# End of the mixers in a hybrid decoder block: the last step's closing traced ahead of the output projection, results stored by GpSimd's queue, the next norm taken operand by operand

## The chip, the cores and the metric

The kernel runs on one core of a Trainium2 chip. A core has five engines with instruction streams of their own: PE (TensorE, matrix products), DVE (VectorE), ACT (ScalarE), POOL (GpSimd) and SP (SyncE, which here only issues transfers). Transfers (DMAs) run on 16 DMA engines that all queues share. The metric is the device time of the whole kernel in microseconds (us). A difference of 0.3%, 9 us, is about what a measurement of this kernel can tell from no change.

## The reference

One decoder layer over 1024 tokens of width 1024, behind 16 meta tokens that are dropped at the end. All is float32.

```
h = [meta; x]
h = h + 0.5 * swiglu(rmsnorm(h), ...)             # first feed-forward block, inner width 2816
u = rmsnorm(h) @ w_in                             # one input projection for both mixers
o_a = gated DeltaNet (8 heads of 128, short causal convolution, chunks)
o_b = RWKV-7 time mixing (16 heads of 64)
h = h + (sigmoid(ga) * o_a + sigmoid(gb) * o_b) @ w_out
h = h + 0.5 * swiglu(rmsnorm(h), ...)             # second feed-forward block
out = rmsnorm(h)[16:]
```

## The kernel before, in words

Activations are kept transposed: 8 row blocks of 128 channels by tokens. Every float32 operand of a large product is split into a high part (`fp32r`, written by ScalarE, L163) and the rest (written by VectorE, L164), and a product is the three matmuls high x high, high x low and low x high. A weight block of 128 x 1024 is loaded into one of two buffers `wraw` by SP, split into one of two buffers `w`, and used by 24 matmuls (`mm3`, L301 to L308; L307 is the matmul).

The kernel has three stages: `ffn1`, `middle` (the mixers) and `ffn2`. The mixers go through two halves of the tokens ("segments", `s` 0 and 1) and in each through 8 channel blocks `j`: 16 steps. The parts of a step (`merge_blocks`, `transitions`, `chains`, `gates`, `finish` and those that prepare later steps) are called in the order of strings such as `FINAL` (L192), which holds for the last step. That order is how the program is written; a scheduler that records all calls then merges them into one instruction stream per engine, by its own estimates of what will be ready. It never reorders on the chip: each engine works through its stream, and a waiting instruction holds all behind it.

The parts around the change:

- `chains` (L1701): short dependent products; the last ones are `bq` (L1773).
- `finish` (L1808) closes a step: square of `oa` and of `yb`, each split into one buffer `hl` (L1226 to L1228), two column sums on TensorE for each (`cs`, L1213), logarithm and exponential (`ro`, `rg`, L1232 and L1234), then VectorE scales and adds (L1815 to L1823). The result `yb` goes to memory (`mdr`) for all steps but the last, whose `yb` is split at once into the operand tile `uk`.
- `fill` (L1035) is the output projection of segment 0. It has no dependence on the last step and fills TensorE beside it. `wout` (L1095) takes a row block `ho` of `h` from memory (L1041), runs 24 matmuls into `pwo` (L307), adds (L1101), and the sum is stored to `h2dr` (L1045). Then it loads the seven merged operands `mr` of segment 1 that lie in memory (L1090) and splits them into `uk` tiles; there are eight of those, so each is free when the last product of segment 0 has read it. `ho` and `mr` share one ring of eight slots (`tmp_tile`), so `mr` number k waits for store number k to have read its slot.
- `ffn2` (L880) loads `h` of segment 0 back from `h2dr` and that of segment 1 from `hdr` into tiles `hh` (L894), whose first 512 columns hold segment 0. `first_half` (L375) runs the norm of segment 0: squares (L320), sums on VectorE (L327), one sum over partitions on TensorE (`nps`, L338), logarithm and exponential (`nrs`, L340 and L341), then per row block a scaling (L381) and a split into `b`. Then the output projection of segment 1 runs (`wout` again, eviction at L1101 into the second 512 columns of `hh`, store to `h3dr`, L898), and `start` runs the norm of segment 1 (squares L363, sums on TensorE L365) beside the first products `pg` of the feed-forward block (L518, later L494).

Of the kernel before, what the change touches and what calls it, by code (L numbers as in the profile page):

```python
# [15 lines left out]
KD = D // P  # L16
# [21 lines left out]
NJ = 8  # L38
# [150 lines left out]
BEFORE_SWITCH = "merge_blocks transitions operands+ inverses+ chains gates finish banks gates+ segment decay++ new_b++ tokens++ new_a++"  # L189
SWITCH = "merge_blocks transitions operands+ inverses+ chains finish decay++ new_b++ new_a++"  # L190
LAST_BUT_ONE = "merge_blocks transitions operands+ inverses+ chains gates finish"
FINAL = "gates merge_blocks transitions chains fill finish"  # L192


def weight_order():
# [179 lines left out]
def first_half(g, hs, gname, n, b, on_pe):  # L375

    src = lambda k: hs[k][:, :n]
    rs = rstd(g, src, n, on_pe)
    yield
    for k in range(KD):  # L380
        g.nc.vector.scalar_tensor_tensor(src(k), src(k), g.V(gname, k), rs, op0=ALU.mult, op1=ALU.mult)  # L381
        bk = b["21" if k >= HK else "11"][:, k % HK]
        split(g, src(k), bk[:, 0, :], bk[:, 1, :])
    yield


def second_half(g, hs, gname, n, b):
# [381 lines left out]
def ffn1(g):  # L769
    tc, nc = g.tc, g.nc  # L770
    n = T // 2
    with ExitStack() as ctx:
# [12 lines left out]
        with tc.tile_pool(name="f1n", bufs=1, reuse_waits="tile") as sp:  # L785
            hs = [sp.tile([P, T], F32, name=f"h{k}") for k in range(KD)]
            for s in range(2):
                for k in range(KD):
                    sl = slice(s * n, (s + 1) * n)
                    (nc.sync if s or k % 2 else nc.scalar).dma_start(hs[k][:, sl], g.a["hT"][k][:, sl])  # L790
                if not s:
                    weight_tiles(g)
                    q0 = whole(g, 1, 0, 0, g.wq[0], g.wq[1])
                    w0 = next(q0)
            q1 = whole(g, 1, 0, 1, g.wq[4], g.wq[2], g.wq[3])
            w1 = next(q1)
            first = first_half(g, hs, "g1", n, b, True)
            next(first)
            next(q0)
            next(first)  # L800
            next(q0)
            start(g, 1, hs, "g1", n, b, (w0, w1), q1)
            gu = g.gate_up
# [76 lines left out]
def ffn2(g):  # L880
    tc, nc = g.tc, g.nc
    n = FULL
    main_banks(g, 1, 6, 8)
    with ExitStack() as ctx:
# [4 lines left out]
        g.ga = ctx.enter_context(tc.tile_pool(name="ga", bufs=1, reuse_waits="tile"))  # L889
        with tc.tile_pool(name="f2n", bufs=1, reuse_waits="tile") as sp:  # L890
            hs = [sp.tile([P, SEQ], F32, name=f"hh{k}") for k in range(KD)]
            for s in range(2):
                for k in range(KD):
                    nc.sync.dma_start(hs[k][:, s * n : (s + 1) * n], g.hdr[1][k] if s else g.h2dr[k])  # L894
            for _ in first_half(g, hs, "g2", n, b, False):
                pass
            for m, ho in wout(g, g.mg, lambda m: hs[m][:, n:]):
                nc.sync.dma_start(g.h3dr[m], ho)  # L898
            g.upctx.close()
            cp = ctx.enter_context(tc.tile_pool(name="f2c", bufs=1, side="right", reuse_waits="tile"))  # L900
            pools.update({x: cp for x in ("t2", "t3", "22", "t4", "t1")})
            b.update({x: cp.tile([P, HK, 2, n], F32R, name=f"b{x}", tag=f"b{x}", bufs=1) for x in pools if x not in b})
            g.wx = right.enter_context(tc.tile_pool(name="wx", bufs=1, side="right", reuse_waits="tile"))
            b["12"] = b["t4"]
            weight_tiles(g)
            q0 = whole(g, 2, 0, 0, g.wq[0], g.wq[1])
            q1 = whole(g, 2, 0, 1, g.wq[4], g.wq[2], g.wq[3])
            w = next(q0), next(q1)
            next(q0)
            next(q0)  # L910
            start(g, 2, hs, "g2", n, b, w, q1)
            gu = g.gate_up
# [122 lines left out]
def fill(g, q):  # L1035

    nc = g.nc

    def add(m):
        ho = tmp_tile(g, "ho")[:, :FULL]  # L1040
        nc.sync.dma_start(ho, g.hdr[0][m][:, SEGS[0][2] :])  # L1041
        return ho

    for m, ho in wout(g, merged(g, 0, range(NJ)), add):
        nc.sync.dma_start(g.h2dr[m], ho)  # L1045
    g.mg = merged(g, 1, range(NJ - 1))


def tmp_tile(g, name, w=528):
# [758 lines left out]
def finish(g, q):  # L1808

    nc, st, V, j = g.nc, g.st, g.V, q.j  # L1810
    oa, yb, zg, gg = q.oa, q.yb, q.zg, q.gg
    sq = q.Va.rearrange("p c m -> p (c m)")
    ro = st.tile([P, FULL], F32, name="ro", tag="ro")
    colsum_rsqrt(g, "ones", oa, sq, ro, FULL, 1.0 / P, V("eps"), pool="ch")
    nc.vector.tensor_tensor(oa, oa, ro, op=ALU.mult)  # L1815
    nc.vector.scalar_tensor_tensor(oa, oa, V("aog"), zg, op0=ALU.mult, op1=ALU.mult)
    sq = q.AR[:, 0:4].rearrange("p c y m -> p (c y m)")
    rg = st.tile([P, FULL], F32, name="rg", tag="ro")
    colsum_rsqrt(g, "bd", yb, sq, rg, FULL, 1.0 / 64, V("gneps"), pool="ch")
    nc.vector.scalar_tensor_tensor(yb, yb, V("lng", j), rg, op0=ALU.mult, op1=ALU.mult)  # L1820
    nc.vector.scalar_tensor_tensor(yb, yb, V("lnb", j), q.bv, op0=ALU.add, op1=ALU.add)
    nc.vector.tensor_tensor(yb, yb, gg, op=ALU.mult)
    nc.vector.tensor_tensor(yb, yb, oa, op=ALU.add)  # L1823
    if q.it + 1 < 2 * NJ:
        nc.sync.dma_start(g.mdr[q.s][j], yb)
    else:
        g.mg.append(u_tile(g, yb))


ACTIONS = {"new_b": new_b, "tokens": tokens, "new_a": new_a, "operands": operands, "inverses": inverses, "merge_blocks": merge_blocks, "transitions": transitions,  # L1830
# [88 lines left out]
```

## Time and profile before

| | |
|---|---|
| median of three runs | 3006.02 us (3003.01 to 3011.42) |
| profiled execution, its own time | 3009.62 us |
| its span in the profile | 3007.6 us |
| TensorE busy | 2890.0 us, 96% of the span |
| VectorE / ScalarE / GpSimd busy | 73% / 48% / 16% |
| DMA, mean | 111 GB/s |
| last step's `bq` to the first `pg` of the second feed-forward block | 2276.9 to 2350.8 us |

A row of the timeline reads: start in us from the span's start, length in us, engine, line, operation, tile written <- tiles read, shape, count, and in brackets the idle time ahead of it with the instruction that ended it. A row of the chain of waits reads: start, length, what; the chain is followed back from the last instruction, at each step to what released it. A float32 product that is no `fp32r` product (the norms' sums) has two rows for each matmul. An instruction's length includes its tail, in which the next may start; where a pace is wanted, starts are compared. SPq and POOLq are transfers at their issue; the data lands later.

### The profile page before, as it was taken

The numbers are of one execution on the slowest core, as the hardware profiler recorded it, in microseconds if no ns is written. First come the engines' busy times: TensorE is split into PE (matmuls) and PEld (weight loads), VectorE is DVE, ScalarE is ACT, GpSimd is POOL, SyncE is SP. The second block draws the span as 40 slices with busy tenths as digits, with TensorE's granted clock in tenths as the row PEclk, the third lists the DMA queues.
The fourth block names the chain that finished last, engine by engine and source line by source line (L and its number), as shares of the span: only waits on it lengthen the run. The fifth ranks groups of instructions, "written<-read, shape, count | busy, mean of one in ns | idle before, by whom it ended". The sixth has DMA issues, their size and how long they took to land.

```text
span 3007.6 us, 62829 instructions
## 1 busy us (share of the span) xinstructions
PE 2890.0 (96%) x25630; PEld 2501.7 (83%) x25630; DVE 2194.8 (73%) x4079; ACT 1445.0 (48%) x2546; POOL 491.2 (16%) x554
## 2 busy tenths in 40 slices
PE   8999999998989999999998999999998999999998
PEld 8999999998878888888776777777776888888886
DVE  7566668776667877788767887777866666667886
ACT  5322234345655656566566656656644432223444
POOL 0332332323000000000000100100100033332531
PEclk9999999999999999999999999999999999999999
DMA  3433236453232322333332332233354333333762
GB/s 123 134 107 106 93 122 210 170 193 111 74 74 66 83 72 64 81 82 87 93 90 71 81 82 75 74 84 86 106 148 158 114 109 103 100 104 132 248 226 95
DMA packets 286849, 333.14 MB, mean 111 GB/s; under 512 B 172432, under 2 KB 178576, under 8 KB 286560
## 3 DMA queue, kind: packets, MB, share of 16 engines
q1 hardware_dynamic: 284752, 325.77, 35.7%
q8 instruction: 201, 3.29, 0.5%
q10 hardware_dynamic: 1728, 3.16, 0.3%
q14 instruction: 88, 0.72, 0.1%
q0 software_dynamic: 80, 0.19, 0.0%
HBM read 261.67 MB, written 67.38 MB: 109 GB/s over the span
## 4 chain that ended last, share of the span: by engine, by line
PE 50%; DVE 12%; ACT 5%; issue 2%; DMA 1%; SPq 0%; POOL 0%; DVEq 0%; ACTq 0%
PE pp L307 16%; PE pg L494 11%; PE pd L707 6%; PE pwo L307 3%; DVE w L164 2%; DVE tb L1581 1%; PE pg L518 1%; DVE Xb L1583 1%; ACT w L163 1%; PE cs L1213 1%; PE vp L1266 1%; PE mp L1266 1%; DVE mt L1689 1%; PE gra L1467 1%; PE np L1266 1%
## 5 line engine op out<-in xcount | busy, mean ns | idle before, releaser
L307 PE MATMUL pp<-uk,w 128*128 128x512 f32 (+2 forms) x4824 | 969.8, 347 | 15.2 <-DVE h L714 6.0
L307 PEld LDWEIGHTS pp<-uk,w 128*128 128x128 f32 x4824 | 744.0, 191 | 111.9 <-DVE w L164 13.1
L707 PE MATMUL pd<-form,w 128*128 128x256 f32 (+2 forms) x2772 | 437.2, 320 | 9.9 <-DVE w L164 9.2
L707 PEld LDWEIGHTS pd<-form,w 128*128 128x128 f32 x2772 | 396.7, 190 | 49.9 <-DVE w L164 12.3
L494 PE MATMUL pg<-bt,w 128*128 128x256 f32 (+2 forms) x2520 | 401.7, 318 | 2.5 <-DVE w L164 2.0
L164 DVE TENSOR_TENSOR w<-wraw,w 128x1024 fp32r<-128x1024 f32 (+2 forms) x266 | 349.2, 1313 | 74.9 <-ACT w L163 71.8
L494 PEld LDWEIGHTS pg<-bt,w 128*128 128x128 f32 x2520 | 360.2, 188 | 36.4 <-DVE w L164 3.1
L163 ACT ACTIVATE w<-wraw 128x1024 fp32r<-128x1024 f32 (+2 forms) x266 | 276.5, 1040 | 191.5 <-PE pg L494 116.1
L500 DVE TENSOR_TENSOR c<-c,pg 128x520 f32<-128x520 f32 (+1 forms) x280 | 189.5, 689 | 240.0 <-PE pg L494 216.0
L494 PE MATMUL pg<-b,w 128*128 128x256 f32 (+2 forms) x2160 | 347.9, 318 | 0.0
L494 PEld LDWEIGHTS pg<-b,w 128*128 128x128 f32 x2160 | 309.8, 188 | 28.0
L163 ACT ACTIVATE w<-wrx 128x1024 fp32r<-128x1024 f32 (+1 forms) x64 | 58.4, 912 | 280.4 <-PE pg L494 238.5
L464 POOL TENSOR_TENSOR wrx<-wrx 128x512 f32<-128x512 f32 x38 | 52.5, 1382 | 727.0 <-DVE w22b L164 549.8
L164 DVE TENSOR_TENSOR form<-form 128x520 fp32r<-128x520 f32 (+1 forms) x152 | 145.1, 991 | 13.0 <-ACT form L163 12.7
L163 ACT ACTIVATE w<-wsum 128x768 fp32r<-128x768 f32 x96 | 75.7, 788 | 160.3 <-PE pd L707 120.9
L164 DVE TENSOR_TENSOR w<-wsum,w 128x768 fp32r<-128x768 f32 x96 | 116.0, 1214 | 36.8 <-ACT w L163 36.8
L1583 DVE TENSOR_TENSOR Xb<-Xb,tb 115x126 f32<-115x126 f32 (+22 forms) x496 | 125.8, 254 | 8.9 <-DVE tb L1581 0.2
L163 ACT ACTIVATE form<-form 128x520 fp32r<-128x520 f32 (+1 forms) x152 | 94.2, 632 | 77.1 <-DMA form<-frm 67.7
L1581 DVE TENSOR_TENSOR tb<-Ub,Xb 115x126 f32<-115x126 f32 (+22 forms) x496 | 124.5, 251 | 8.4 <-DMA Ub<-scr 1.2
L242 POOL TENSOR_TENSOR wsum<-wsum,wraw 128x768 f32<-128x768 f32 (+1 forms) x48 | 96.3, 2020 | 209.7 <-DMA wraw<-in_wdn 122.1
L1390 DVE SCALAR_TENSOR_TENSOR acc<-xr,pk,acc 128x528 f32<-128x528 f32 (+1 forms) x144 | 108.9, 757 | 28.5 <-ACT acc L1386 28.0
L307 PE MATMUL pwo<-uk,w 128*128 128x512 f32 x384 | 99.5, 412 | 4.1 <-DVE w L164 1.9
(424 smaller groups left out, 4391.3 us busy)
## 6 DMA issues: line engine op xcount, KB each, us to landing
wraw<-in_win SPq DMA_DIRECT2D x150, 512.0 KB
wraw<-in_wgu SPq DMA_DIRECT2D x44, 512.0 KB
wrx<-in_wgu SPq DMA_DIRECT2D x44, 512.0 KB
frm<-c SPq DMA_DIRECT2D x76, 260.0 KB
form<-frm SPq DMA_DIRECT2D x76, 260.0 KB
frm<-c SPq DMA_DIRECT2D x76, 256.0 KB
form<-frm SPq DMA_DIRECT2D x76, 256.0 KB
wraw<-in_wdn SPq DMA_DIRECT2D x40, 384.0 KB
```

The costliest lines, as they stand in the source:

```text
L163: g.nc.scalar.activation(hi, src, AF.Copy)
L164: (eng or g.nc.vector).tensor_tensor(lo, src, hi.bitcast(F32), op=ALU.subtract)
L242: g.nc.gpsimd.tensor_tensor(s, x, y, op=ALU.add if r == 1 else ALU.subtract)
L307: g.nc.tensor.matmul(ps, lhsT=l, rhs=r, start=i == 0, stop=i == n - 1)
L464: sums.tensor_tensor(a22, a21, a22, op=ALU.add)
L494: nc.tensor.matmul(ps[:, c0 : c0 + cn], lhsT=l[:, x, k, :], rhs=r[:, k, y, c0 : c0 + cn], start=i == 0, stop=i == 3 * HK - 1)
L500: nc.vector.tensor_tensor(o, x, y, op=ALU.add)
L707: nc.tensor.matmul(pd[:, c0 : c0 + cn], lhsT=wd[:, u, k - k0, :], rhs=x[:, v, c0 : c0 + cn], start=k + i == 0, stop=k == HF - 1 and i == 2)
L1266: g.nc.tensor.matmul(ps[e][HS[dst], c0 : c0 + CB], lhsT=l, rhs=r, start=True, stop=True)
L1390: nc.vector.scalar_tensor_tensor(acc[:, :n], xr[:, tap : tap + n], V("convw", ct * 4 + tap), acc[:, :n], op0=ALU.mult, op1=ALU.add)
L1581: nc.vector.tensor_tensor(tv, U[:, i, i + 1 :].unsqueeze(2).to_broadcast([npt, nt, ncc]), X[:, i, 0:ncc].unsqueeze(1).to_broadcast([npt, n ...
L1583: nc.vector.tensor_tensor(X[:, i + 1 :, 0:ncc], X[:, i + 1 :, 0:ncc], tv, op=ALU.add)
```

## The change

Four edits:

1. In the last step `finish` is called before `fill`, not behind it. The last `yb` is kept (`g.last`) and split into its `uk` tile at the end of `fill`.
2. The stores to `h2dr` and `h3dr` and the reload of `h2dr` go through GpSimd's queue instead of SP's.
3. In `ffn2` the loads of segment 1's `h` (`hdr`) come ahead of segment 0's.
4. `first_half` yields after every row block, and in `ffn2` it is advanced within the loop of the second projection: the norm's sums after row block 1, then two row blocks of scaling and splitting in each of row blocks 2 to 5. In `ffn1` it is run to its end at the place where it was.

```
-FINAL = "gates merge_blocks transitions chains fill finish"
+FINAL = "gates merge_blocks transitions chains finish fill"
...
     for k in range(KD):
         g.nc.vector.scalar_tensor_tensor(src(k), src(k), g.V(gname, k), rs, op0=ALU.mult, op1=ALU.mult)
         bk = b["21" if k >= HK else "11"][:, k % HK]
         split(g, src(k), bk[:, 0, :], bk[:, 1, :])
-    yield
+        yield
...
-            next(first)
+            for _ in first:
+                pass
...
-            for s in range(2):
-                for k in range(KD):
-                    nc.sync.dma_start(hs[k][:, s * n : (s + 1) * n], g.hdr[1][k] if s else g.h2dr[k])
-            for _ in first_half(g, hs, "g2", n, b, False):
-                pass
+            for k in range(KD):
+                nc.sync.dma_start(hs[k][:, n:], g.hdr[1][k])
+            for k in range(KD):
+                nc.gpsimd.dma_start(hs[k][:, :n], g.h2dr[k])
+            first = first_half(g, hs, "g2", n, b, False)
             for m, ho in wout(g, g.mg, lambda m: hs[m][:, n:]):
-                nc.sync.dma_start(g.h3dr[m], ho)
+                nc.gpsimd.dma_start(g.h3dr[m], ho)
+                if m:
+                    next(first, None)
+                    if m > 1:
+                        next(first, None)
...
     for m, ho in wout(g, merged(g, 0, range(NJ)), add):
-        nc.sync.dma_start(g.h2dr[m], ho)
-    g.mg = merged(g, 1, range(NJ - 1))
+        nc.gpsimd.dma_start(g.h2dr[m], ho)
+    g.mg = merged(g, 1, range(NJ - 1)) + [u_tile(g, g.last)]
...
-        g.mg.append(u_tile(g, yb))
+        g.last = yb
```

What the scheduler makes of it is seen in the streams. Up to the last step they are the same but for line numbers (the changed kernel's are 1 higher behind `ffn1`'s call of `first_half`, and 5 higher behind `ffn2`'s projection loop).

TensorE's stream from `bq`, the last product of the chains, to the next feed-forward block, before:

```order
L1773 MATMUL bq<-AR,SBs 64x64 x16
L307 MATMUL pwo<-uk,w 128x512 x35
L1213 MATMUL cs<-hl,onesr 128x512 x2
L1213 MATMUL cs<-hl,bdr 128x512 x2
L307 MATMUL pwo<-uk,w 128x512 x73
L338 MATMUL nps<-nsq,ones 128x512
L307 MATMUL pwo<-uk,w 128x512 x23
L365 MATMUL nps<-nsq,ones 128x512 x2
L307 MATMUL pwo<-uk,w 128x512 x2
L365 MATMUL nps<-nsq,ones 128x512
L307 MATMUL pwo<-uk,w 128x512 x94
L365 MATMUL nps<-nsq,ones 128x512 x5
```

And in the changed kernel:

```order
L1778 MATMUL bq<-AR,SBs 64x64 x16
L1218 MATMUL cs<-hl,onesr 128x512
L307 MATMUL pwo<-uk,w 128x512 x2
L1218 MATMUL cs<-hl,onesr 128x512
L307 MATMUL pwo<-uk,w 128x512 x11
L1218 MATMUL cs<-hl,bdr 128x512
L307 MATMUL pwo<-uk,w 128x512 x4
L1218 MATMUL cs<-hl,bdr 128x512
L307 MATMUL pwo<-uk,w 128x512 x77
L338 MATMUL nps<-nsq,ones 128x512
L307 MATMUL pwo<-uk,w 128x512 x130
L365 MATMUL nps<-nsq,ones 128x512 x8
```

The closing's column sums move from behind 35 projection matmuls to among the first 17, three matmuls go ahead of `bq`, and all eight norm sums of segment 1 stand behind the projection.

ScalarE's stream in the same place, from the square of `yb` on, before (`w` is a weight's split, `uk<-mr` that of a loaded operand; rows at L1226, L1227, L1232 and L1234 are the closing):

```order
L1226 ACTIVATE AR<-yb 128x512
L163 ACTIVATE w<-wraw 128x1024
L163 ACTIVATE uk<-mr 128x512 x6
L163 ACTIVATE w<-wraw 128x1024
L1232 ACTIVATE ro<-cs,pk 128x512
L163 ACTIVATE uk<-mr 128x512
L1234 ACTIVATE ro<-ro 128x512
L1227 ACTIVATE hl<-yb 128x512
L1232 ACTIVATE rg<-cs,pk 128x512
L1234 ACTIVATE rg<-rg 128x512
L163 ACTIVATE uk<-yb 128x512
L163 ACTIVATE w<-wraw 128x1024
```

And in the changed kernel:

```order
L1237 ACTIVATE ro<-cs,pk 128x512
L1231 ACTIVATE AR<-yb 128x512
L1239 ACTIVATE ro<-ro 128x512
L1232 ACTIVATE hl<-yb 128x512
L163 ACTIVATE w<-wraw 128x1024
L163 ACTIVATE uk<-mr 128x512 x2
L1237 ACTIVATE rg<-cs,pk 128x512
L163 ACTIVATE uk<-mr 128x512
L1239 ACTIVATE rg<-rg 128x512
L163 ACTIVATE uk<-mr 128x512 x4
L163 ACTIVATE w<-wraw 128x1024
L163 ACTIVATE uk<-yb 128x512
```

The closing's instructions move ahead of the operands that come from memory, and the last of those now stands between them and the split of `yb`.

SP's stream from the store of row block 5 to the reloads, before:

```order
L1045 DMA h2dr<-ho 128x512
L260 DMA wraw<-in_wout 128x1024
L1090 DMA mr<-mdr_86 128x512
L1045 DMA h2dr<-ho 128x512
L260 DMA wraw<-in_wout 128x1024
L1090 DMA mr<-mdr_86 128x512
L1045 DMA h2dr<-ho 128x512
L260 DMA wraw<-in_wout 128x1024
L894 DMA hh_27542<-h2dr 128x512
```

In the changed kernel SP's stream in this place (the transfers of `hh` are now those of segment 1):

```order
L1095 DMA mr<-mdr_86 128x512 x4
L260 DMA wraw<-in_wout 128x1024
L1095 DMA mr<-mdr_86 128x512
L260 DMA wraw<-in_wout 128x1024
L1095 DMA mr<-mdr_86 128x512 x2
L260 DMA wraw<-in_wout 128x1024
L894 DMA hh_27542<-hdr_84 128x512
```

And GpSimd's stream, which before had only the two copies here:

```order
L1765 COPY SBs<-SB 128x64
L1050 DMA h2dr<-ho 128x512 x3
L1602 COPY XA<-Xc 32x4x32 x2
L1050 DMA h2dr<-ho 128x512 x5
L896 DMA hh_27542<-h2dr 128x512
```

The stores no longer stand between SP's loads; the first reload stands behind the last store, and all eight reloads ahead of the first store to `h3dr`.

## The prediction

> **What bounds the kernel now.** I read the page first: which engine is full over the whole span.
>
> ```profile
> span 3007.6 us, 62829 instructions
> PE 2890.0 (96%) x25630; PEld 2501.7 (83%) x25630; DVE 2194.8 (73%) x4079; ACT 1445.0 (48%) x2546; POOL 491.2 (16%) x554
> ```
>
> TensorE is busy for 96% of the span, so time can only be won where it stands still or runs at a low clock. All that moves lies between the last step of the chains and the first product of the second feed-forward block. So I read TensorE's timeline there (start, length, instruction, in brackets the idle time ahead of it and who ended it).
>
> ```profile
> 2276.80 8.23 PE L307 MATMUL pwo<-uk,w 128*128 128x512 f32 x35
> 2284.86 0.63 PE L1213 MATMUL cs<-hl,onesr 128*128 128x512 f32 x2
> 2288.58 1.68 PE L1213 MATMUL cs<-hl,bdr 128*128 128x512 f32 x2 [3.09 <-ACT hl L1227]
> 2291.04 18.38 PE L307 MATMUL pwo<-uk,w 128*128 128x512 f32 x73 [0.78 <-ACT rg L1232]
> 2309.25 1.03 PE L338 MATMUL nps<-nsq,ones 128*128 128x512 f32 x2
> 2309.72 5.82 PE L307 MATMUL pwo<-uk,w 128*128 128x512 f32 x23
> ...
> 2320.06 0.73 PE L307 MATMUL pwo<-uk,w 128*128 128x512 f32 x2 [1.48 <-ACT w L163]
> 2322.65 23.88 PE L307 MATMUL pwo<-uk,w 128*128 128x512 f32 x92 [1.86 <-DVE w L164]
> 2346.37 4.45 PE L365 MATMUL nps<-nsq,ones 128*128 128x512 f32 x10
> ```
>
> Four waits, in two pairs: 3.09 + 0.78 around the column sums of the closing (`finish`), and 1.48 + 1.86 = 3.34 us at weights of the second projection; 7.21 us together. Next the granted clock (the columns after the length are the busy times of PE, PEld, DVE, ACT and POOL, then the clock, the DMA share and GB/s).
>
> ```profile
> 2288.00:2294.00 6.00, 4.55 (x9) 2.96 (x10) 4.29 (x8) 1.84 (x4) 0.00 (x0) 0.50 0.96 321
> 2294.00:2302.00 8.00, 8.00 (x35) 6.57 (x35) 3.83 (x5) 4.28 (x7) 0.00 (x0) 0.98 0.96 341
> 2322.00:2328.00 6.00, 5.35 (x13) 4.21 (x14) 2.94 (x4) 0.76 (x2) 0.00 (x0) 0.50 0.68 204
> ```
>
> After each pair TensorE gets half its clock for some 6 us. A wait here is paid twice: once standing, once slow. The Trainium skill ("TensorE: Matmul & The Clock Gate", Part 1) has the gate fall to half after an idle window of about 3.4 us; here pairs of 3.87 and 3.34 us, with a few matmuls between, were enough. The sums below take the clock from the rows alone.
>
> How much is there to win? The chain of waits gives matmuls at full pace and the place where the next block starts:
>
> ```profile
> 2220.59 18.81 PE pwo L307 x83
> 2276.86 2.73 PE pwo L307 x11
> ...
> 2346.53 4.29 PE nps L365 x10
> 2350.82 5.26 PE pg L518 x23
> ```
>
> A projection matmul takes 18.81 / 83 = 0.227 us. Between 2276.86 and 2350.82, 73.96 us, stand 35 + 192 = 227 of them (51.4 us), four column sums (0.23 us each by the same pace, 0.9) and nine matmuls for the norms at 4.29 / 5 = 0.86 us (7.7; each has two rows in the trace). That is 60.0 us of work. So 13.9 us are lost: 7.2 standing and 6.7 slow. This is the most that the change can give.
>
> Why the first pair waits is in the same chain, a few pieces earlier:
>
> ```profile
> 2281.97 0.33 SPq L260
> ...
> 2282.65 4.19 DMA mr<-mdr
> ...
> 2286.86 0.64 ACT uk L163
> ```
>
> ScalarE holds the closing's square (`hl` L1227) behind the split of the seventh loaded operand `mr`. That load sits in SP's queue behind a weight load and, through its slot, behind a store of `h2dr`. The closing itself needs none of this.
>
> **The change part by part.**
>
> *The closing ahead of the fill.* On ScalarE the closing's square, logarithms and exponentials now stand ahead of the loaded operands, and TensorE gets its sums 0, 2, 13 and 17 matmuls after `bq` (L1773) instead of after 35. Nothing is added: the same 192 + 192 projection matmuls, three of them moved ahead of `bq`, so that `bq` ends about 0.7 us later (2277.5) and 224 follow it. I walk the closing with lengths from these rows (ScalarE then VectorE, per piece: a split of 512 is 3.75 / 6 and 3.69 / 6, about 0.53 and 0.60 from start to start; a weight split 0.96 and 1.14; a VectorE step of the closing 0.60 to 0.75).
>
> ```profile
> 2279.62 1.06 ACT L163 ACTIVATE w<-wraw 128x1024 fp32r<-128x1024 f32 x1 [0.81 <-PE pwo L307]
> 2280.59 3.75 ACT L163 ACTIVATE uk<-mr 128x512 fp32r<-128x512 f32 x6
> 2280.71 1.23 DVE L164 TENSOR_TENSOR w<-wraw,w 128x1024 fp32r<-128x1024 f32 x1 [0.40 <-ACT w L163]
> 2281.86 3.69 DVE L164 TENSOR_TENSOR uk<-mr,uk 128x512 fp32r<-128x512 f32 x6
> 2292.47 0.75 DVE L1821 SCALAR_TENSOR_TENSOR yb<-yb,pk,bv 128x512 f32<-128x512 f32 x1
> ```
>
> The first sums end at 2278.5; logarithm, square, exponential and split on ScalarE end near 2280.9, when TensorE has done the 13 projection matmuls between (2277.5 + 2 x 0.23 + 13 x 0.227 = 2280.9). The second part of `hl` is ready at 2281.7, four matmuls are done at 2282.1: no wait. So 3.09 + 0.78 us and their half clock go.
>
> *What is late next there.* The second projection starts when the fill ends, at 2277.5 + 0.9 + 32 x 0.227 = 2285.7, and takes an operand every 3 x 0.227 = 0.68 us. VectorE must by then have split eight operands and run the closing between them: by the walk operands 3 and 4 come 0.45 and 0.5 us late, the last (`yb`) just in time near 2291.4. I charge 1.0 us. The seventh `mr` waits for the slot that the store of row block 6 frees; that store leaves at 2280.5 from GpSimd. With 2 us for the store (SP waited that long for such a store) and the 4.19 us above, the operand is there at 2287, and needed at 2290.9.
>
> ```profile
> SPq L1090 <- DMA h2dr<-ho: 2.0, 1, 2.0
> pk<-in_pk POOLq DMA_DIRECT2D x1, 126.0 KB, 6.0
> ones<-in_ck POOLq DMA_DIRECT2D x1, 64.0 KB, 5.1
> ```
>
> With the 6.0 us of GpSimd's own queue instead it is 2291.4, and the wait grows to some 3 us: the upper end. Lower end: 0.
>
> *Stores and reloads on GpSimd's queue.* 24 transfers (8 stores `h2dr`, 8 reloads into `hh`, 8 stores `h3dr`) leave SP, where each costs 0.32 to 0.43 us. GpSimd idles there:
>
> ```profile
> L894 SPq DMA_DIRECT2D hh<-h2dr x8: 319/422/430, 2287.8 to 2293.2; - x8
> 2236.95 0.69 DVE L1101 TENSOR_TENSOR ho<-pwo,ho 128x512 f32<-128x512 f32 x1 [3.07 <-PE pwo L307]
> 1.27 0.71 POOL L128 DMA_DIRECT2D ones<-in_ck  x1 [0.81 <-POOLq L1909]
> 1.98 0.54 POOL L130 DMA_DIRECT2D pk<-in_pk  x1
> 2238.76 0.99 POOL L1597 COPY XA<-Xc 32x128 f32<-32x128 f32 x2 [38.11 <-DMA Xc<-scX]
> 2246.94 0.76 PE L1635 MATMUL iv<-XA,UA 64*64 64x64 f32 x8
> 2416.46 1.29 POOL L464 TENSOR_TENSOR wrx<-wrx 128x512 f32<-128x512 f32 x1 [176.71 <-DVE w22b L164]
> ```
>
> Its only work between 2240 and 2416 us is what the change puts there, so issuing costs nothing by itself. Queued behind three stores is the copy `XA` at 2238.76; the third store is free at 2237.6, so the copy slips by under 1 us, and its reader (L1635) starts at 2246.9: hidden.
>
> The price is the order in that queue. Reload 0 stands behind store 7, and store 7 waits for the fill's last eviction, now at 2287.2 on VectorE. Eight reloads at 0.71 us leave by 2293.6. From 2283.5 on the 16 transfers of 256 KB and four weight blocks of 512 KB, 6.3 MB, share about 345 GB/s (the window rows: 321 and 341), that is 18 us; the reloads, a third of it, end when two queues share evenly at about 2300. Squares and additions follow at 0.54 and 0.61 us a piece:
>
> ```profile
> 2299.31 2.70 ACT L320 ACTIVATE nsq<-hh 128x512 f32<-128x512 f32 x5
> 2300.58 3.06 DVE L327 TENSOR_TENSOR nsq<-nsq 128x512 f32<-128x512 f32 x4
> ```
>
> The last is added near 2302.1. TensorE reaches the norm's sum (now 77 matmuls after the last closing sum) at 2282.4 + 77 x 0.227 + 1.0 = 2300.8. I charge 1.4 us. Lower end 0 (reloads that land 4.2 us after their issue: 2297.8); upper end 6 us: issue stretched as GpSimd's work is stretched in this trace, 2.15 against 1.29 us, gives 1.2 us each, the last issued at 2297 and landing 6.0 us later, done at 2304.5, 3.7 us late, and 2 us of half clock.
>
> ```profile
> 2417.83 1.29 POOL L465 TENSOR_TENSOR wrx<-wraw,wrx 128x512 f32<-128x512 f32 x1
> 2420.58 2.15 POOL L467 TENSOR_TENSOR wraw<-wraw 128x512 f32<-128x512 f32 x1
> ```
>
> *First norm operand by operand.* Before, VectorE scales and splits eight operands in one burst and the weight splits queue behind it (waits of 1.48 and 1.86 us). Now two operands stand per product of 24 matmuls (5.4 us), in which VectorE has 2 x (0.66 + 0.60) us for them, 1.14 for a weight and 0.6 for an eviction: 4.3 us. So 3.34 us and their half clock go. Behind the last product eight norm matmuls run instead of five; three moved, none added, and the eighth waits for one eviction and square (1.2 us) that seven others (6 us) cover. The first feed-forward block issues the same instructions: zero.
>
> **Sum.** 13.9 won, less 1.0 and 1.4: 11.5 us. The profiled execution took 3009.62 us around its span of 3007.6; the median of the runs is 3006.02, and the change acts on either alike: 3006.0 - 11.5 = 2994.5, say 2995 us. With both lower ends 2992, with both upper ends (3 with 2 of half clock, and 6) about 3003.
>
> **Rivals.**
>
> *Late reloads (some of the gain is given back).* For it: they queue behind store 7, in the stretch where the DMA share is 0.96. Against: by the walk they miss by only 1.4 us. By the upper ends 13.9 - 5 - 6 = 3 us remain; 2998 to 3004.
>
> *Slower: GpSimd's queue runs its transfers one after another.* The two rows at the start cannot show whether their landings overlap (5.1 and 6.0 us for issues 0.7 us apart suggest that they do). If each reload waited for the one before, eight at 5.1 us from 2288 end at 2329, 28 us after TensorE needs them; less the 13.9, the kernel takes 3006 + 14 = 3020 us. It decides from 2.9 us a reload: 2288 + 8 x 2.9 = 2311.2, with square and addition 11.7 us late, and 2 us of half clock after it.
> The Trainium skill ("SBUF — State Buffer", "SBUF: two separate sides") has a rule that speaks against the change: descriptors of GpSimd's transfers are not written while VectorE runs an instruction that takes both ports, and it tells of a 620 ns transfer that took 3100 ns. At 3.1 us each, an estimate from that page, the reloads would end near 2313 and the time be about 3007 to 3009. VectorE's rows in this stretch are two-operand TENSOR_TENSORs, no plain copies, so by that rule the trap stays open; no run here shows it yet.
>
> *No change: the waits only move.* If the seventh operand and the closing's last are late together (store and load at 6 + 4.2 us), the pair of waits returns at the start of the second projection, 3 us and 3 of half clock, and the reloads lose what remains: 3004 to 3007.
>
> **Chances.** Gain as summed, 2991 to 2998: 0.60. Late reloads, 2998 to 3004: 0.24. Waits that only move: 0.08. Slower: 0.08. The bound of what a measurement can tell is 0.3%, 9 us, so faster means under 2997.0. The summed case lies below it but for a small part of 0.05, so faster 0.55; within it 0.39; slower than 3015 0.06. The range of 2990 to 3005 holds the first two cases and leaves out the ends of both.
>
> **What would show it.** In the profile after: no wait over 1 us at the column sums (the closing right); the wait ahead of the norm's sum L338 under 3 us and the clock at 1.0 beside it (the reloads right); no wait at weights in the 130 matmuls behind (operand by operand right); GpSimd's issues near 0.7 us each. From `bq`'s end to the next block's first product there should be 62 to 63 us instead of 74. A wait of over 5 us for a reload of `hh`, or a half clock in this stretch, makes the prediction wrong.

## The result, and the profile after

| | before | changed |
|---|---|---|
| median | 3012.36 us (20 runs) | 3001.75 us (20 runs) |
| range of single runs | 3003.01 to 3018.53 us | 2994.87 to 3016.43 us |
| ratio, 95% interval | | 0.9974 (0.9964 to 0.9983) |
| profiled execution, span | 3009.62, 3007.6 us | 2995.63, 2993.9 us |
| stretch: start of `bq` to start of the first `pg` | 74.54 us | 64.54 us |

By the ratio the change saves 7.8 us (0.26% of 3012.36; 5.1 to 10.8 by the interval); the plain medians lie 10.6 us apart. A second comparison (again, below) gives 7.2 and 5.7. Predicted were 2995 us and a gain of 11.5. The time lies in the range; the gain is smaller than forecast, and 11.5 lies outside its interval. It is less than the 9 us given above as what a measurement can tell, but with 20 runs of each kernel the interval leaves out zero. The span of the profiled execution is 13.7 us shorter, but only 10.0 us of that lie in the stretch; the rest is scatter, since the same kernel reaches `bq` anywhere between 2273 and 2283 us in the profiles below.

Page of the changed kernel, its first lines:

```profile
span 2993.9 us, 62859 instructions
PE 2885.6 (96%) x25630; PEld 2498.0 (83%) x25630; DVE 2188.1 (73%) x4079; ACT 1444.1 (48%) x2546; POOL 507.6 (17%) x578
```

TensorE's timeline of the changed kernel in the stretch (start, length, instruction, idle time ahead and who ended it):

```profile
2273.62 1.15 PE L1778 MATMUL bq<-AR,SBs 64*64 64x64 f32 x32
...
2279.61 0.39 PE L1218 MATMUL cs<-hl,bdr 128*128 128x512 f32 x1
2279.84 5.87 PE L307 MATMUL pwo<-uk,w 128*128 128x512 f32 x25
2286.09 0.98 PE L307 MATMUL pwo<-uk,w 128*128 128x512 f32 x3 [0.38 <-DVE uk L164]
2287.29 11.43 PE L307 MATMUL pwo<-uk,w 128*128 128x512 f32 x49 [0.23 <-DVE uk L164]
2301.22 1.13 PE L338 MATMUL nps<-nsq,ones 128*128 128x512 f32 x2 [2.50 <-DVE nsq L327]
2301.78 30.07 PE L307 MATMUL pwo<-uk,w 128*128 128x512 f32 x130
...
2338.16 19.62 PE L518 MATMUL pg<-b,w 128*128 128x512 f32 x84
```

Both pairs of waits are gone, at the column sums (3.09 + 0.78) and at the weights (1.48 + 1.86), with the half clock behind them. What is left is 0.61 us at operands and 2.50 us ahead of the norm's sum L338. The chain of waits of the changed kernel says why that sum waits:

```profile
2285.13 6.17 DMA h2dr<-ho
2291.30 0.28 issue
2291.58 8.14 DMA hh<-h2dr
...
2299.81 0.64 ACT nsq L320
...
2300.47 0.70 DVE nsq L327
...
2301.22 1.13 PE nps L338 x2
```

The last reload reads what the last store writes. That store takes 6.17 us to land, the reload 8.14 more. The windows of the changed kernel (stretch, its length, then busy time of PE, PEld, DVE, ACT and POOL, the granted clock, the DMA share and GB/s) show the crowd of transfers they are in:

```profile
2284.00:2288.00 4.00, 3.40 (x14) 2.17 (x13) 4.00 (x8) 1.56 (x2) 2.74 (x6) 1.00 0.99 335
...
2296.00:2300.00 4.00, 2.72 (x12) 1.91 (x11) 2.84 (x5) 1.80 (x4) 0.54 (x1) 1.00 1.03 405
```

All 16 DMA engines are full from 2284 to 2300 us: the share is 0.99 to 1.04 in each of the four windows of 4 us. GpSimd's timeline of the changed kernel has the eight reloads at 0.54 to 0.55 us each and the last one held:

```profile
2285.66 3.87 POOL L896 DMA_DIRECT2D hh<-h2dr  x7
2291.58 0.54 POOL L896 DMA_DIRECT2D hh<-h2dr  x1 [2.05 <-DMA h2dr<-ho]
```

And ScalarE's has the squares, each waiting for its reload (the sixth and the last of the eight):

```profile
2297.22 0.63 ACT L320 ACTIVATE nsq<-hh 128x512 f32<-128x512 f32 x1 [0.87 <-DMA hh<-h2dr]
...
2299.81 0.63 ACT L320 ACTIVATE nsq<-hh 128x512 f32<-128x512 f32 x1 [0.67 <-DMA hh<-h2dr]
```

### The profile page after: what moved, and what is told of

Read it like the earlier page. It is cut to its first block, busy times and chain, and to the rows that moved or that the text cites. A ratio compares the mean times of both kernels' runs of the same rounds, so it can differ in the third digit from the quotient of the medians.

```text
span 2993.9 us, 62859 instructions
## 1 busy us (share of the span) xinstructions
PE 2885.6 (96%) x25630; PEld 2498.0 (83%) x25630; DVE 2188.1 (73%) x4079; ACT 1444.1 (48%) x2546; POOL 507.6 (17%) x578
## 4 chain that ended last, share of the span: by engine, by line
PE 47%; DVE 12%; ACT 5%; issue 3%; DMA 3%; SPq 1%; POOL 0%; DVEq 0%; ACTq 0%; POOLq 0%
PE pp L307 16%; PE pg L494 11%; PE pd L707 4%; PE pwo L307 2%; DVE w L164 2%; DVE tb L1586 1%; PE pg L518 1%; DVE Xb L1588 1%; ACT w L163 1%; DMA form<-frm 1%; PE vp L1271 1%; PE cs L1218 1%; PE mp L1271 1%; DVE mt L1694 1%; PE gra L1472 1%
```

## The experiments

Each ratio is against the kernel before on the same chip (again2 is a profile alone). The stretch is that of one profile. "Closing" is the sum of TensorE's waits at and behind the column sums of `finish`, "norm's sum" its wait ahead of L338, and "weights" is the sum of TensorE's waits at splits of `w` in the second projection.

| kernel | stretch | closing | norm's sum | weights | ratio (95%) |
|---|---|---|---|---|---|
| before | 74.5 | 3.87 | 0 | 3.34 | |
| changed | 64.5 | 0 | 2.50 | 0 | 0.9974 (0.9964 to 0.9983) |
| null | 74.2 | 4.04 | 0 | 3.33 | 0.9996 (0.9985 to 1.0008) |
| again, again2 | 67.2, 65.6 | 0 | 3.56, 3.47 | 0 | 0.9976 (0.9965 to 0.9988) |
| order_only | 72.8 | 0 | 0 | 5.89 | 1.0004 (0.9991 to 1.0018) |
| queue_only | 65.6 | 3.26 | 0 | 0 | 0.9981 (0.9970 to 0.9991) |
| norm_only | 67.5 | 4.03 | 0 | 0 | 0.9985 (0.9973 to 0.9998) |
| all_on_sp | 68.7 | 0 | 0 | 3.61 | 0.9985 (0.9975 to 0.9994) |
| queue_order | 69.4 | 0 | 2.95 | 0 | 0.9986 (0.9973 to 0.9999) |
| h3_only | 73.1 | 3.78 | 0 | 2.91 | 0.9994 (0.9983 to 1.0006) |
| h2_only | 65.8 | 3.26 | 0 | 0 | 0.9984 (0.9969 to 1.0000) |
| burst_m3 | 75.5 | 3.71 | 0 | 3.96 | 1.0001 (0.9988 to 1.0014) |
| norm_later | 64.6 | 0 | 1.28 | 0.53 | 0.9966 (0.9952 to 0.9980) |
| late_hdr | 63.4 | 0 | 1.30 | 0 | 0.9969 (0.9958 to 0.9980) |
| both_later | 62.5 | 0 | 0.31 | 0 | 0.9959 (0.9945 to 0.9973) |

**The parts alone.** First the closing ahead of the fill, and nothing else (order_only):

```
-FINAL = "gates merge_blocks transitions chains fill finish"
+FINAL = "gates merge_blocks transitions chains finish fill"
...
-    g.mg = merged(g, 1, range(NJ - 1))
+    g.mg = merged(g, 1, range(NJ - 1)) + [u_tile(g, g.last)]
...
-        g.mg.append(u_tile(g, yb))
+        g.last = yb
```

> Only the closing ahead of the fill; stores, reloads and the first norm as before. Stretch meant: from the end of bq to the first product of the second feed-forward block, 74.0 us before and 63.9 after the whole change. Theory (two separate pairs of waits, each paid again at half clock): the pair at the column sums goes (3.9 us and some 3 of half clock), the pair at the weights behind the burst of scaling and splitting stays (3.3 and some 3): stretch 66 to 68, whole time 6 to 8 us less than before. Rival (SP's queue, with stores between its loads, is what held the closing up): the wait only moves to the operands of the second projection, stretch 72 to 74, no change.

TensorE's timeline of order_only behind the norm's sum:

```profile
2300.45 3.11 PE L307 MATMUL pwo<-uk,w 128*128 128x512 f32 x11
...
2309.68 1.22 PE L307 MATMUL pwo<-uk,w 128*128 128x512 f32 x2 [4.41 <-ACT w L163]
2311.16 1.22 PE L307 MATMUL pwo<-uk,w 128*128 128x512 f32 x2 [0.25 <-ACT w L163]
2313.61 29.27 PE L307 MATMUL pwo<-uk,w 128*128 128x512 f32 x116 [1.23 <-DVE w L164]
```

The closing's waits go as forecast, but the stretch is 72.8 us where 66 to 68 were expected: the waits at weights grow from 3.34 to 5.89 us. The reason is in the stream. The norm's sum now stands 12 matmuls earlier in the second projection, and only 11 stand behind it, not 23, before a weight that is split behind the burst. These matmuls are called the burst's cover from here on.

Then the queue alone, edits 2 and 3 of the change (queue_only):

```
-            for s in range(2):
-                for k in range(KD):
-                    nc.sync.dma_start(hs[k][:, s * n : (s + 1) * n], g.hdr[1][k] if s else g.h2dr[k])
+            for k in range(KD):
+                nc.sync.dma_start(hs[k][:, n:], g.hdr[1][k])
+            for k in range(KD):
+                nc.gpsimd.dma_start(hs[k][:, :n], g.h2dr[k])
...
-                nc.sync.dma_start(g.h3dr[m], ho)
+                nc.gpsimd.dma_start(g.h3dr[m], ho)
...
-        nc.sync.dma_start(g.h2dr[m], ho)
+        nc.gpsimd.dma_start(g.h2dr[m], ho)
```

> Only the queues: stores to h2dr and h3dr and the reload of h2dr on GpSimd's queue, loads of segment 1 first; closing behind the fill and the norm in one burst as before. Theory (order of ScalarE's stream holds the closing): the seventh operand comes some 2 us earlier, the wait at the column sums shrinks by that but stays over 1 us, the burst's waits at weights stay: stretch 70 to 73, whole time 1 to 4 us less. Rival (the queue is the cause): the column sums wait less than 0.5 us and the stretch is 67 or less.

TensorE's timeline of queue_only:

```profile
2285.99 0.50 PE L1214 MATMUL cs<-hl,bdr 128*128 128x512 f32 x1 [2.82 <-ACT hl L1228]
2286.92 0.80 PE L1214 MATMUL cs<-hl,bdr 128*128 128x512 f32 x1 [0.44 <-DVE hl L1229]
2287.51 17.27 PE L307 MATMUL pwo<-uk,w 128*128 128x512 f32 x70
2304.61 1.02 PE L338 MATMUL nps<-nsq,ones 128*128 128x512 f32 x2
2305.07 12.36 PE L307 MATMUL pwo<-uk,w 128*128 128x512 f32 x52
```

The closing's pair stays, the weights' pair is gone, though the burst is as long as ever. At 65.6 us the stretch lies below what was expected and below the rival's 67 too. The part that the prediction priced at no gain of its own takes 9 us out of the stretch. The third part alone (norm_only: edit 4, with reloads and stores on SP) takes the weights' pair away as well:

```
-    yield
+        yield
...
-            for _ in first_half(g, hs, "g2", n, b, False):
-                pass
+            first = first_half(g, hs, "g2", n, b, False)
...
+                if m:
+                    next(first, None)
+                    if m > 1:
+                        next(first, None)
```

> Only the first norm operand by operand within the second projection; closing behind the fill, all transfers on SP as before. Theory: the two waits at weights (1.48 and 1.86 us) and the half clock behind them go, the pair at the column sums stays: stretch 67 to 69, whole time 5 to 7 us less. Rival (the burst was hidden, the waits came from late weight loads): waits at weights stay, stretch 73 to 74.

TensorE's timeline of norm_only behind the sums of segment 1's norm, with no wait at a weight:

```profile
2324.16 21.92 PE L307 MATMUL pwo<-uk,w 128*128 128x512 f32 x94
```

Both give 7 to 9 us in the stretch, and the ratios agree with that within their intervals (queue_only 5.7 us, 2.7 to 9.0; norm_only 4.5, 0.6 to 8.1). With the closing behind the fill, either alone is enough for the second pair. All of the change but the queue (all_on_sp: the diffs of order_only and norm_only together):

> The changed order and the norm operand by operand, but all stores and reloads on SP's queue as before. Theory (order does nearly all, GpSimd's queue is worth little): stretch 62 to 65, whole time within 3 us of the changed kernel's, 8 to 11 us less than before. Rival (stores between SP's loads hold operands, reloads and weights up): a wait of over 3 us comes back in the stretch, 67 us or more, whole time 3 to 6 us above the changed kernel's.

The rival's case came true. TensorE's timeline of all_on_sp behind the norm's sum:

```profile
2298.81 3.10 PE L307 MATMUL pwo<-uk,w 128*128 128x512 f32 x11
...
2308.04 0.73 PE L307 MATMUL pwo<-uk,w 128*128 128x512 f32 x2 [3.01 <-ACT w L163]
2309.38 28.66 PE L307 MATMUL pwo<-uk,w 128*128 128x512 f32 x118 [0.60 <-DVE w L164]
```

The weights wait 3.61 us again, with 11 matmuls of cover as in order_only. The operands are recorded two per row block, but in VectorE's stream five of them stand in front of the next weight's split (from 2301.18 to 2308.11 us), so a shorter burst is left. The parts are therefore no sum: -1.8, -9.0 and -7.0 us in the stretch alone, together -7.4 to -10.0.

**What moves the weights' pair.** The reading after these four was that weight loads stand behind waiting stores in SP's queue. Two halves of the queue's move test it. h3_only moves the stores to `h3dr` alone:

```
-                nc.sync.dma_start(g.h3dr[m], ho)
+                nc.gpsimd.dma_start(g.h3dr[m], ho)
```

> The kernel before, with only the stores to h3dr moved to GpSimd's queue. Theory (in SP's queue the weight loads of the second projection stand behind stores to h3dr that wait for its evictions): the waits at weights L163 and L164 (1.5 and 1.9 us) and the half clock behind them go, the pair at the column sums (about 3.1 and 0.8 us) stays, stretch 67 to 69 us of the kernel before's 74.5; ratio 0.998. Rival (the weights are late because stores to h2dr and the reloads of hh stand ahead of them and fill the DMA engines): the waits at weights stay above 1 us each, stretch 73 to 75, ratio 1.000.

h2_only is the diff of queue_only without that line:

> The kernel before, with the stores to h2dr and their reloads on GpSimd's queue (segment 1's h loaded first) and the stores to h3dr still on SP's. Theory (only the stores to h3dr hold the weight loads up): waits of 3 us or more in sum stay at the weights, and the pair at the column sums stays, stretch 72 to 75, ratio 0.9995 to 1.000. Rival (it is the stores to h2dr and the reloads that hold the weight loads up): no wait over 1 us at weights, stretch 66 to 69, ratio 0.998.

Both came out against the theory. In h3_only the two weight loads leave SP from 2303.71 us on, 25 us after the start of `bq`, where before they left 35 us after it (2310.36), and TensorE waits all the same, for VectorE's half of the split. VectorE's and then TensorE's timeline of h3_only:

```profile
2323.80 1.22 DVE L164 TENSOR_TENSOR w<-wraw,w 128x1024 fp32r<-128x1024 f32 x1
```

```profile
2312.74 6.28 PE L307 MATMUL pwo<-uk,w 128*128 128x512 f32 x25
...
2325.07 22.74 PE L307 MATMUL pwo<-uk,w 128*128 128x512 f32 x92 [2.91 <-DVE w L164]
```

The split stands behind the burst in VectorE's stream, wherever its load is. VectorE's timelines of the kernel before and then of h2_only around the burst:

```profile
2304.88 1.23 DVE L164 TENSOR_TENSOR w<-wraw,w 128x1024 fp32r<-128x1024 f32 x1 [1.24 <-ACT w L163]
...
2311.86 2.08 DVE L381 SCALAR_TENSOR_TENSOR hh<-hh,pk,nrs 128x512 f32<-128x512 f32 x3 [1.94 <-ACT nrs L341]
...
2321.38 1.22 DVE L164 TENSOR_TENSOR w<-wraw,w 128x1024 fp32r<-128x1024 f32 x1
```

```profile
2302.39 1.22 DVE L164 TENSOR_TENSOR w<-wraw,w 128x1024 fp32r<-128x1024 f32 x1
...
2308.69 1.23 DVE L164 TENSOR_TENSOR w<-wraw,w 128x1024 fp32r<-128x1024 f32 x1 [0.51 <-ACT w L163]
2309.84 2.07 DVE L381 SCALAR_TENSOR_TENSOR hh<-hh,pk,nrs 128x512 f32<-128x512 f32 x3
...
2319.95 1.22 DVE L164 TENSOR_TENSOR w<-wraw,w 128x1024 fp32r<-128x1024 f32 x1
```

In h2_only one more weight is split, in the pause before the burst that the kernel before stands idle in (1.94 us). Then 50 matmuls (11.4 us) stand behind the norm's sum before a weight from behind the burst is needed, and the burst of some 10 us hides; before, it was 23 (5.2 us). To try this without a queue, burst_m3 leaves all transfers on SP and records the whole burst behind row block 3:

```
-            for _ in first_half(g, hs, "g2", n, b, False):
-                pass
+            first = first_half(g, hs, "g2", n, b, False)
...
+                if m == 3:
+                    for _ in first:
+                        pass
```

> The kernel before with all its transfers on SP's queue and the eight norm operands still in one burst, but the burst is recorded behind row block 3 of the second projection, so that three weight splits of the projection stand ahead of it in VectorE's stream, not two. Theory (the pair of waits at the weights is a matter of place in VectorE's stream: behind two splits the burst of 9.3 us outlasts the cover, behind three it does not): the 1.5 and 1.9 us at weights go or fall under 0.5 us each, stretch 66.5 to 69 us, ratio 0.998. Rival (the weight loads themselves come too late through SP's queue): ScalarE's split L163 waits for its load, TensorE waits 2 us or more at the same weights, stretch 71 to 75, ratio 0.9995 to 1.000.

A miss: three splits stand ahead now, but the norm's sum moved by a product too, so its cover is 24 matmuls, about as before, and 0.77 + 3.19 us are waited. So the number of splits does not decide; the cover fits these runs. Over the kernels with the whole burst: 11 matmuls 5.89 us, 23 matmuls 3.34 and 2.91, 24 matmuls 3.96, 34 matmuls none (queue_order, below), 50 matmuls none (queue_only, h2_only). No run changed the cover and nothing else, so this is the reading that fits, not one that was tried by itself. Why the scheduler finds the place for one more split when the `h2dr` transfers leave SP was not tried; it orders by its own estimates.

queue_order has the closing and the queue, with the burst (the diffs of order_only and queue_only together):

> The closing ahead of the fill and GpSimd's queue, while the norm's eight operands are still scaled and split in one burst. Theory (the waits at weights came from weight loads behind waiting stores in SP's queue, not from the burst): no wait over 1 us at weights L163 or L164 in the second projection, stretch 64 to 66 us, the same as the changed kernel within 1 us. Rival (the prediction's: the burst holds the weight splits up): waits of 1.5 us and more at weights behind the norm's sum, with half clock after them, stretch 68 to 71.

No wait at weights (34 matmuls of cover), as the first theory had it, but 69.4 us: the evictions `hh` L1102 stand behind the burst, a sum of segment 1's norm waits 2.44 us for one of them, and L338 waits 2.95. Against the changed kernel's three profiles (mean 65.8) operand by operand is worth 3.6 us here, by one profile of queue_order.

**How late the reloads are.** The kernel before and the changed kernel once more:

> The kernel before, unchanged, as a yardstick. If the profiles tell the stretch from bq to the first pg well, it is again 73 to 75 us here (74.5 before), with waits of about 3 us at the column sums and about 3 us at weights, and the ratio is 1.000 within 0.001. If the stretch of the kernel before varies from one execution to the next, for instance because transfers land at other times, its waits come out by 2 us or more different, and then differences of that size between the other kernels' profiles mean nothing.

> The changed kernel, unchanged. Theory (the change is worth what the stretch shows, and the whole shows it too once enough runs are compared): ratio 0.996 to 0.9975, stretch 64 to 65.5 us against the kernel before's 74, wait ahead of the norm's sum L338 1 to 3 us. Rival (something outside the stretch gives part of the gain back): stretch as said, but the ratio stays at 0.998 or more, and a place behind pg L518 is longer by 2 to 3 us in each profile of this kernel.

> The changed kernel a third time, for its profile. Theory (the reloads land at times that differ by a microsecond or two from one execution to the next, so the wait ahead of the norm's sum L338 is anywhere from 2 to 4 us and the stretch from 64 to 67.5): a wait of 2 to 4 us; half clock behind it where it is over 3.4 us, none where it is under 3. Rival (2.5 us is the rule and 3.6 was an accident): 2.3 to 2.7 us, stretch 64.3 to 65.

The stretch of before repeats within 0.4 us, that of the changed kernel does not: 64.5, 67.2 and 65.6. TensorE's row at L338 and a window behind it, of again:

```profile
2304.58 2.07 PE L338 MATMUL nps<-nsq,ones 128*128 128x512 f32 x2 [3.56 <-DVE nsq L327]
```

```profile
2304.50:2308.00 3.50, 3.42 (x6) 2.06 (x7) 1.25 (x2) 2.56 (x4) 0.00 (x0) 0.53 0.00 0
```

The same two of again2:

```profile
2311.59 1.13 PE L338 MATMUL nps<-nsq,ones 128*128 128x512 f32 x2 [3.47 <-DVE nsq L327]
```

```profile
2311.50:2315.00 3.50, 3.40 (x13) 2.50 (x14) 2.02 (x3) 2.58 (x4) 0.00 (x0) 1.00 0.01 2
```

The wait is 3.2 us in the mean of three, and once the half clock comes behind it. The mean stretch, 65.8 against 74.4 before, gives 8.6 us, and the two comparisons of whole runs 7.8 and 7.2 by their ratios.

Two ways to take this wait away. norm_later puts the norm's sum and the operands one row block later:

```
-                if m:
+                if m > 1:
                     next(first, None)
-                    if m > 1:
+                    if m > 2:
                         next(first, None)
```

> As the changed kernel, but the norm's sum and the scaled operands come one row block later in the second projection. Theory (the 2.5 us ahead of the norm's sum are the late reloads of hh behind store 7 in GpSimd's queue, ready at a fixed time): the sum now stands 10 matmuls, 2.3 us, later and waits 0 to 0.6 us; stretch 61.5 to 63 us, 1.5 to 2.5 less than the changed kernel. Rival (VectorE is full here, and what comes later in the projection is missing at its end): waits of 1 to 3 us turn up at the norm sums L365 or at the first pg, whose operands b are late, and the stretch stays at 64 to 66.

The sum stands 2.3 us later and waits 1.28, about what 3.5 less 2.3 leaves, where up to 0.6 was expected; 0.53 us are waited at a weight. Against the changed kernel's own 64.5 to 67.2 the stretch of 64.6 is no clear gain. late_hdr leaves the sum 1.1 us later and moves transfers that are not yet wanted behind the reloads:

```
-            for k in range(KD):
+            for k in range(3):
                 nc.sync.dma_start(hs[k][:, n:], g.hdr[1][k])
             for k in range(KD):
                 nc.gpsimd.dma_start(hs[k][:, :n], g.h2dr[k])
+            for k in range(3, KD):
+                nc.gpsimd.dma_start(hs[k][:, n:], g.hdr[1][k])
```

> The changed kernel, with five of the eight loads of segment 1's h (row blocks 3 to 7) moved from SP's queue to GpSimd's, behind the reloads of h2dr; the norm's sum comes 5 matmuls, 1.1 us, later in the stream. Theory (the reloads land late because the DMA engines are full, at a share of 1.0, from 2284 to 2300 us, and 1.3 MB of that isn't wanted yet; at 400 GB/s that is 3.3 us): the last reload lands 2 to 3.5 us earlier after bq, the wait ahead of the norm's sum L338 falls from 2.5 and 3.6 us to 0 to 0.5, stretch 61.5 to 63 us, ratio 0.995 to 0.9965. Rival (a reload on GpSimd's queue has a pace of its own, 1.3 to 1.5 us apart, whatever else moves): they land at the same times, the wait falls by the 1.1 us alone, to 1.4 to 2.5 us, stretch 64 to 66.

GpSimd's and then ScalarE's timeline of late_hdr:

```profile
2291.14 4.39 POOL L896 DMA_DIRECT2D hh<-h2dr  x8
```

```profile
2296.59 2.18 ACT L320 ACTIVATE nsq<-hh 128x512 f32<-128x512 f32 x4
2299.18 1.42 ACT L320 ACTIVATE nsq<-hh 128x512 f32<-128x512 f32 x2 [0.41 <-DVE nsq L327]
2302.89 1.06 ACT L163 ACTIVATE w<-wraw 128x1024 fp32r<-128x1024 f32 x1 [2.30 <-DMA wraw<-in_wout]
2303.86 1.14 ACT L320 ACTIVATE nsq<-hh 128x512 f32<-128x512 f32 x2
```

All eight reloads leave in one row, so the last one no longer waits for the last store, and no square waits for a reload any more. The sixth starts by 20.9 us after the start of `bq` (2279.08), against 23.6 in the changed kernel: the crowd was the reason, as the theory had it. But the last two squares stand behind a weight whose load is late in the same crowd (2.30 us), so 1.30 us are left where up to 0.5 was expected. both_later joins the two diffs:

> The changed kernel with both postponements: the norm's sum and operands one row block later (10 matmuls, 2.3 us) and five of the loads of segment 1's h behind the reloads on GpSimd's queue. Theory (what still costs in the changed kernel is the lateness of the reloads, 2.5 to 3.6 us at the norm's sum, and each postponement takes part of it): no wait over 0.5 us at the norm's sum L338 or at weights, stretch 61.5 to 62.5 us, ratio 0.995 to 0.9965. Rival (what comes later in the projection is missing at its end, or a weight load behind the crowd of transfers is late): a wait of 1 us or more at weights or at the first pg, stretch 63.5 or more, no better than either postponement alone (64.6 and 63.4).

TensorE's timeline of both_later at the norm's sum:

```profile
2303.08 1.12 PE L338 MATMUL nps<-nsq,ones 128*128 128x512 f32 x2 [0.31 <-DVE nsq L327]
2303.64 27.81 PE L307 MATMUL pwo<-uk,w 128*128 128x512 f32 x120
```

62.45 us from `bq` to `pg`, inside what was expected, and a median of 2998.07 us against 3010.04; by the ratio 12.3 us less than before (8.1 to 16.6). This is the best version found; its lead over the changed kernel itself was not measured with the two in one comparison.

## Where the prediction was right, and where it was wrong

- *The closing ahead of the fill.* Right in its place: no wait at the column sums, 0.61 us at operands where 1.0 was charged, the seventh operand in time. Wrong in its worth. By itself it gains nothing that could be measured (order_only): the burst keeps less cover, and with the weights mended it is the reloads that are waited for. Half of the reason for the pair did not hold either. ScalarE's order did hold the closing's square up, but not through a late load: in the kernel before the seventh operand's split waits 0.16 us for its load (ScalarE's row below), and in queue_only and norm_only, where it does not wait at all, the pair is still 3.26 and 4.03 us. queue_only keeps the closing's pair and has the stretch of the whole change (65.6 against 65.8).

```profile
2286.86 0.63 ACT L163 ACTIVATE uk<-mr 128x512 fp32r<-128x512 f32 x1 [0.16 <-DMA mr<-mdr]
```

- *The stores and reloads: the step that failed.* "I charge 1.4 us" for the norm's sum; it measured 2.50, 3.56 and 3.47, with 1.5 us more at half clock in the second (0.5 at the sum, 1.0 in the 130 matmuls behind). The walk let eight reloads leave back to back behind the last store, and end in an even share of the crowd; it put nothing on the landing of that store, which the eighth reload has to wait for. In the trace the two stand one behind the other: 6.17 us for the store, of which the reload waits 2.05 at its issue, and 8.14 for the reload, which then lands with the last of the crowd (2299.72), not ahead of it. Counted from the end of `bq`, the last addition ends 26.4 us later (2301.17 less 2274.77), where the walk had 24.6 (2302.1 less 2277.5). The walk's own figures leave 1.2 us, not 1.4: 2282.4 + 77 x 0.227 + 1.0 is 2300.9. Edit 3 belongs to the cause: it put segment 1's loads ahead of the reloads, and late_hdr, which takes five of the eight back, makes the reloads earlier. The wait that the prediction named as its first rival, late reloads, took a good part of what it left over. By its own signs (under 3 us at L338, no half clock) the reloads passed in the first profile and failed in the next two. The price of issue was too high (0.54 us each for 0.71), and nobody waits for it.
- *Operand by operand.* Its reason, the burst that outlasts the cover, stands: norm_only removes the pair, and h3_only and burst_m3 keep it with the loads early or the splits moved. Wrong was that it alone does so, and always: the queue's move brings the second pair down as well, by a changed place in VectorE's stream, which the prediction did not read, and in all_on_sp the pair is there in spite of it.
- *The sum.* 11.5 us, measured 7.8 (5.1 to 10.8). Stretch: 63.0 forecast (74.5 less 11.5); 65.8 in the mean of three. Of the 2.8 us between, 1.8 are the reloads' wait (3.2 against 1.4), 0.5 the half clock shared over three profiles, and 0.4 are given back by the operands; the rest, 0.9, is a pace of 0.230 us a matmul in the 130 behind the sum where 0.227 was used (0.4) and small gaps. both_later, without that wait, gives the 62.45 us and the 12.3 us that the sum promised.
- *The base: the second step that failed.* The three runs shown had a median of 3006.02; 20 runs give 3012.36, later groups 3009.9 to 3011.0. So 2995 was low by 6.8 us mostly because its base was 6.3 too low: by the plain medians the gain is only 0.9 too large, by the ratio 3.7. That the time still lies in the range is owed to the range's width.
- *The slower rival.* Refuted: the reloads overlap. In the changed kernel the sixth one's square starts 11.6 us after the first one's issue (2297.22 less 2285.66), while one after another at 5.1 us six would need 30.

## What to carry to other kernels

A wait that is taken off the path is worth what the next late thing leaves of it: walk on to the following two or three waits, and ask for each whether its time is set by TensorE's arrival or, like a store that is read back from memory, by something that does not move. Where a burst on one engine lies in the stream, count the matmuls that cover it before a piece behind it is needed, and read that from the streams. Transfers that nobody wants yet belong behind those that somebody waits for, also across queues, since all share the same engines.

## What the runs showed that was not expected

- In these rows the clock behind a wait is no function of its length. Ahead of L338, 2.50 us left it at 1.00, 2.95 us brought 0.70 (queue_order, the window below), 3.47 us left it at 1.00 (again2), and 3.56 us brought 0.53 (again). The Trainium skill ("TensorE: Matmul & The Clock Gate", Part 1) has the clock fall after an idle window of about 3.4 us, and the window runs free of the program. That the window runs free would fit rows as close as 3.47 and 3.56 us with such different ends. The 2.95 us do not fit: they are shorter than the window and were followed by half clock all the same.

```profile
2307.00:2311.00 4.00, 3.26 (x8) 2.23 (x9) 2.50 (x3) 3.27 (x5) 0.00 (x0) 0.70 0.16 62
```

- GpSimd issued a transfer of 256 KB in 0.54 us each time, also while VectorE was busy for 4.00 of 4 us (2284 to 2288), against 0.32 to 0.43 on SP in the kernel before. The Trainium skill ("DMA: Bandwidth & Descriptors", Issuing engines are not separate DMA queues) has all transfers share the same 16 engines, whoever starts them, so that another issuer only saves issue time. The crowd at a share of 1.0 agrees; the 9 us of queue_only do not come from issue time: they go with the changed place of a weight's split in VectorE's stream.
- With all 16 engines full the rate was 400 to 405 GB/s from 2288 to 2300 us of the changed kernel; the prediction used 345, from windows of before with a share of 0.96. It did not save the forecast, as the reloads came last.
